# Experts' slabs of 1024 columns, down rows in pairs, and weight splits emitted ahead in a hybrid attention and mixture-of-experts kernel

## The chip, the cores and the metric

The kernel runs on one core of one Trainium2 chip. The metric is device time in microseconds (us), the median of three runs. All times below are us unless marked ns.

## The reference

Two layers over 256 tokens of width 1024, in float32. Layer 0 is an attention of two kinds of heads and a SwiGLU of width 2816. Layer 1 is a gated MLP and a mixture of 8 experts with 2 experts per token. Each half layer ends in a residual sum and a layer norm. The change is in the experts:

```python
D_MODEL = 1024; SEQ = 256; N_EXPERTS = 8; TOP_K = 2; D_FF_EXPERT = 3584
...
logits = (xf @ w_router).astype(jnp.float32)
top_val, top_idx = lax.top_k(logits, TOP_K)
gate = jax.nn.softmax(top_val, axis=-1)
...
def expert_block(args):
    xb, e = args
    return (jax.nn.silu(xb @ w_gate[e]) * (xb @ w_up[e])) @ w_down[e]
...
contrib = yb[dest] * g_sorted[:, None].astype(yb.dtype)
y = jnp.zeros((n_tok, dm), yb.dtype).at[tok_sorted].add(contrib)
```

`w_gate[e]` and `w_up[e]` have 1024 rows and 3584 columns, `w_down[e]` 3584 rows and 1024 columns: 336 MB (2^20 bytes each) of weights for the eight experts, all of which are read.

## The kernel before

Every weight is used as two float32r parts whose sum is the float32 value: `wh`, the rounded value, and `wl`, the rest. `weights` (L94) loads a tile of 128 partitions x 2048 floats (1 MB) into a raw buffer through SyncE's queue (L108), copies it to `wh` on the scalar engine, ACT (L123), and subtracts `wh` from it on the vector engine, DVE, or on GpSimd, POOL, to get `wl` (L127). `MOE_CUTS` (1, 1) does each in one instruction. Raw buffers form a ring: 4 in `stream`, 7 in `late`, 1 in `late2` and `W_BUFS_MOE` = 2 in the experts' pool, 14 in all; the first expert tiles also pass through the room of `xhl1` and `yacc` before these are needed. Split tiles form a ring of `WS_BUFS` = 3. An activation is split in the same way (`split_into`, L132: a copy on ACT, a subtraction on DVE), and each product becomes three on TensorE: high by high, high by low, low by high.

An expert has 128 slots for tokens. `gather` (L828) picks the tokens' rows with a 0/1 matrix (`take`) by products on TensorE, and splits them into `xh` and `xl`. The expert's 3584 hidden columns are worked in 7 slabs of 512. For each slab `expert_up` (L852) takes two tiles of gate weights and two of up weights (512 rows x 512 columns each) into one PSUM bank per matrix (`ps_a`, 4 banks), with tokens as the stationary operand; silu on ACT (L865) and a multiplication on DVE (L866) give `sg` [token, column]. `expert_turn` (L869) turns it with four transposes into a `ps_t` bank (2 banks) and splits it into `hh` and `hl` (`tag` with one buffer each). `expert_down` (L878) multiplies with two tiles of 256 rows of `w_down` into two banks that are kept for the whole expert; it runs one slab late, so that slab s + 1's gate and up products stand between the turn of slab s and its use.

After an expert's last slab `combine` (L895) splits the two banks into `y`, spreads them to the tokens' places with products L904 and L905 into `ps_t`, scales them on ACT into `part` (L910, one buffer of both token blocks) and adds them to `yacc` on POOL (L911). This stands in the middle of the next expert's first slab. The last expert adds on DVE instead and goes on into the last norm (`finish`).

Nothing sets an order by hand in this stage but the order of emission: each engine has one queue, a scheduler fills it at build time in order of emission as far as its own account of what is ready allows, and at run time each queue is worked strictly in its order. `run_experts` (L958) has the first two tiles split by POOL, and two more on DVE, while the router still works; `GATE_SLAB` = 3 and `GATHER_SLAB` = 5 say behind which slab the gate weights and the next expert's gather are emitted. A loop behind it (L999) treats experts with more tokens than slots; the trace shows no pass of it.

Of the kernel before, what the change touches and what calls it, by code (L numbers as in the profile page):

```python
# [17 lines left out]
P = 128  # L18
T = 256
# [15 lines left out]
W_BUFS, W_BUFS_LATE, W_BUFS_MOE, WS_BUFS = 4, 7, 2, 3  # L35
MOE_CUTS = (1, 1)
# the order of the attention's parts, and what takes the low parts of each part's weights: the vector engine or gpsimd
# [3 lines left out]
# how many of a group's four heads the scalar engine scales, for each block of queries  # L41
ASIDE = dict(a=(1, 1), w=(0, 1), s=(2, 1))
GATE_SLAB, GATHER_SLAB = 3, 5
# [7 lines left out]
def tile_hybrid_gmlp_moe(  # L51
# [23 lines left out]
    # weights: rings of 8 KB buffers (raw, and the two parts), spread over the pools that exist at the time  # L75
# [13 lines left out]
    def room(shape, dtype=F32):  # L89
        """a tile in the next buffer of the ring for raw weights"""  # L90
        pool, n = slot("w")
        return pool.tile(shape, dtype, name="w", tag="w", bufs=n)

    def weights(src, a, b, lo_engine=V, loads=1, cuts=(2, 4), behind=None):  # L94
        """src as two float32r parts whose sum is src; loaded and split in as many pieces as asked for, each equal
        share of the pieces queued behind what one entry of behind has for their engine."""
# [80 lines left out]
    def norm_rows(z, gb, state, to=None, done=None):  # L177
        """z [t, D], whose halves' statistics are in state -> its norm, in place or in to; done is called with each
        half after it."""
# [11 lines left out]
    def layer_norm(z, gb, accs=None, ready=None, done=None):  # L191
        """z [t, D] -> its norm, in place; with accs, z is first ALPHA * z plus the two halves in accs.
        ready is called with each half before the norm."""
# [9 lines left out]
    def mm_rows(accs, lhs_h, lhs_l, parts, first, last, done=None):  # L203
        """accs[b][half][t, 512] += x[:, k]^T w[k]; parts: (wh, wl, row chunks) of weight tiles, one block at a time."""
# [18 lines left out]
    def rows_2k(w, g, lo_engine=V):  # L223
        """rows g * 256 to g * 256 + 255 of a matrix of D columns"""
        return weights(w[g * 256:(g + 1) * 256, :].rearrange("(k p) c -> p k c", p=P), 2, D, lo_engine)
# [6 lines left out]
    def mm_cols(acc, lhs_h, lhs_l, w, js):  # L232
        """acc[col, t] = w[:, js]^T x, over the whole model dimension."""
# [13 lines left out]
    with ExitStack() as actx:  # L247
# [4 lines left out]
        # bias tables: -slope * distance, masked  # L252
# [7 lines left out]
        # compressed keys: token t against the last position of window c  # L260
# [14 lines left out]
        # sel[r, c] = 1 where r is c or c + 32: adds the two parts of a stacked product  # L275
# [41 lines left out]
        # softmax of one group of four heads over dense keys: probabilities times `scale4`, transposed  # L317
# [123 lines left out]
        # compression of k and v: two products around a gelu, for the 15 windows of each head  # L441
        def compress(lo_engines):
            for i, w1 in enumerate((cmp_wk1, cmp_wv1)):
# [16 lines left out]
                # gelu(z) = z / (1 + exp(-2 sqrt(2 / pi) (z + 0.044715 z^3)))  # L460
# [83 lines left out]
        # projections and attention, in the order that keeps the tensor engine fed  # L544
# [22 lines left out]
        # output projection, residual, norm  # L567
# [15 lines left out]
    with ExitStack() as fctx:  # L583
# [29 lines left out]
        def ffn_up_blocks(s):  # L613
            """the same, one block of tokens after the other"""
# [53 lines left out]
    with ExitStack() as gctx:  # L668
# [14 lines left out]
        # with the norm's gain and shift taken into the weights, it works from what the norm is taken of  # L683
# [42 lines left out]
        def route(b, zt, mv, rs):  # L726
            """zt: what the norm of this block is taken of, transposed"""
# [17 lines left out]
        def rank_tokens():  # L745
            """rank[t, b, e]: how many earlier tokens the expert has; -1 where the token isn't the expert's"""
# [69 lines left out]
    # the ring goes on in what was the last layer's; the room of the sums takes a weight tile first  # L816
# [11 lines left out]
    def gather(n, take):  # L828
        """the rows of x that the slots take, transposed and split; and the way back, [slot, t]"""
# [16 lines left out]
    n_slab = FE // 512  # L846

    def up_weights(w, s, kh, *how, **kw):
        src = w[kh * 512:(kh + 1) * 512, s * 512:(s + 1) * 512]
        return weights(src.rearrange("(k p) c -> p k c", p=P), 4, 512, *how, **kw)  # L850

    def expert_up(w_gate, w_up, s, xh, xl, ready):  # L852
        pss = []
        for w in (w_gate, w_up):
            acc = ps_a()
            for kh in range(2):
                wh, wl = ready.pop(0) if ready else up_weights(w, s, kh, cuts=MOE_CUTS)
                for i in range(4):
                    k = 4 * kh + i
                    PE.matmul(acc, xh[:, k, :], wh[:, i, :], start=k == 0, stop=False)  # L860
                    PE.matmul(acc, xh[:, k, :], wl[:, i, :], start=False, stop=False)  # L861
                    PE.matmul(acc, xl[:, k, :], wh[:, i, :], start=False, stop=k == KD - 1)  # L862
            pss.append(acc)
        sg = moe.tile([P, 512], F32, name="sg", tag="sg", bufs=1)
        S.activation(sg, pss[0], AF.Silu)  # L865
        V.tensor_tensor(sg, sg, pss[1], op=OP.mult)  # L866
        return sg
# [175 lines left out]
```

## Time and profile before

| | us |
|---|---|
| median of three runs (lowest, highest) | 1482.59 (1481.17, 1483.14) |
| the profiled execution: its span, from its first to its last instruction (the time known of it) | 1480.9 |
| TensorE products busy | 1426.8 (96%) |
| DVE busy | 1182.6 (80%) |
| ACT busy | 953.0 (64%) |
| POOL busy | 174.3 (12%) |

One execution was profiled. Its span is 1.7 us below the median. "Busy" of TensorE (PE) is the time in which at least one product is under way; products overlap, and their ends are modelled, so the pace must be read from starts. PEld is the load of the stationary operand, which runs beside the products. A queue row (SPq) is the issue of a DMA, not its transfer. The first expert's products start at 448 us, the last product of the kernel at 1464.8 us.

### The profile page before, as it was taken

How to read it: one execution, taken by the hardware profiler on the slowest of the kernel's cores; microseconds unless marked ns; L12 is line 12 of the kernel's file. 1: busy time of each engine (PE TensorE's matmuls, PEld its weight loads, DVE VectorE, ACT ScalarE, POOL GpSimd, SP SyncE). 2: the span in 40 equal slices, each digit the busy share in tenths (PEclk: the TensorE clock that was granted, in tenths of full speed). 3: DMA queues.
4: the chain of work that ended last, by engine and by line, in shares of the span. 5: the costliest groups of instructions: out<-in, count | busy, mean ns of one | idle time of the engine just before them, and what ended most of it. 6: DMA issues, size and time to landing. Idle time of an engine off the chain costs nothing. (4 is left out here: it accounts for less than half of the span.)

```text
span 1480.9 us, 18693 instructions
## 1 busy us (share of the span) xinstructions
PE 1426.8 (96%) x7207; PEld 1186.0 (80%) x7207; DVE 1182.6 (80%) x1265; ACT 953.0 (64%) x920; POOL 174.3 (12%) x139
## 2 busy tenths in 40 slices
PE   8899999999979999999999999999999999999995
PEld 7887899997768887888788788878878887887883
DVE  7888855558667988888888888888888878888886
ACT  5677544443436767776776777777677667767772
POOL 8521100002050101000200200020020002002000
PEclk9999999999989999999999999999999999999998
DMA  9523975556558898999999999999999999999940
GB/s 274 175 88 98 351 261 185 198 171 214 179 190 295 313 358 312 358 364 329 328 364 342 330 351 361 346 328 368 339 325 365 363 335 331 363 351 323 353 191 31
DMA packets 198847, 425.72 MB, mean 287 GB/s; under 512 B 8472, under 2 KB 44368, under 8 KB 198752
## 3 DMA queue, kind: packets, MB, share of 16 engines
q1 hardware_dynamic: 196448, 419.71, 80.2%
q0 software_dynamic: 1248, 4.24, 1.0%
q8 instruction: 58, 0.95, 0.3%
q10 hardware_dynamic: 1056, 0.53, 0.1%
q14 instruction: 37, 0.30, 0.1%
HBM read 423.40 MB, written 1.05 MB: 287 GB/s over the span
## 5 line engine op out<-in xcount | busy, mean ns | idle before, releaser
L127 DVE TENSOR_TENSOR wl<-w,wh 128x2048 fp32r<-128x2048 f32 (+1 forms) x544 | 907.4, 1696 | 189.3 <-ACT wh L123 185.8
L123 ACT CAST wh<-w 128x2048 fp32r<-128x2048 f32 (+1 forms) x462 | 766.5, 1668 | 255.9 <-PE ps_a L862 102.3
L860 PE MATMUL ps_a<-wh,xhl 128*128 128x512 f32 x896 | 356.4, 398 | 0.0
L862 PE MATMUL ps_a<-wh,xhl 128*128 128x512 f32 x896 | 354.4, 396 | 0.0
L861 PE MATMUL ps_a<-wl,xhl 128*128 128x512 f32 x896 | 354.2, 395 | 0.0
L862 PEld LDWEIGHTS ps_a<-wh,xhl 128*128 128x128 f32 x896 | 168.4, 188 | 39.5
L861 PEld LDWEIGHTS ps_a<-wl,xhl 128*128 128x128 f32 x896 | 168.5, 188 | 38.5
L860 PEld LDWEIGHTS ps_a<-wh,xhl 128*128 128x128 f32 x896 | 168.4, 188 | 38.6
L892 PE MATMUL ps_d<-wl,hh 128*128 128x512 f32 x448 | 178.8, 399 | 0.0
L893 PE MATMUL ps_d<-wh,hl 128*128 128x512 f32 x448 | 176.8, 395 | 0.0
L891 PE MATMUL ps_d<-wh,hh 128*128 128x512 f32 x448 | 167.7, 395 | 0.4 <-ACT hh L133 0.4
L911 POOL TENSOR_TENSOR yacc<-yacc,part 128x512 f32<-128x512 f32 x28 | 65.4, 2356 | 796.9 <-ACT part L910 796.9
L236 PE MATMUL ps_a<-xth,wh 128*128 128x256 f32 x448 | 128.6, 288 | 3.1 <-DVE hg L471 3.1
L238 PE MATMUL ps_a<-xth,wl 128*128 128x256 f32 x448 | 128.5, 287 | 0.8 <-DVE wl L127 0.8
L237 PE MATMUL ps_a<-xtl,wh 128*128 128x256 f32 x448 | 127.7, 285 | 0.0
L891 PEld LDWEIGHTS ps_d<-wh,hh 128*128 128x128 f32 x448 | 84.2, 188 | 20.9 <-ACT hh L133 0.9
L892 PEld LDWEIGHTS ps_d<-wl,hh 128*128 128x128 f32 x448 | 84.3, 188 | 20.1 <-DVE wl L127 1.4
L893 PEld LDWEIGHTS ps_d<-wh,hl 128*128 128x128 f32 x448 | 84.3, 188 | 18.5
L236 PEld LDWEIGHTS ps_a<-xth,wh 128*128 128x128 f32 x448 | 86.5, 193 | 4.9 <-issue 3.7
L238 PEld LDWEIGHTS ps_a<-xth,wl 128*128 128x128 f32 x448 | 86.5, 193 | 2.5 <-issue 1.2
L237 PEld LDWEIGHTS ps_a<-xtl,wh 128*128 128x128 f32 x448 | 86.5, 193 | 0.9 <-DVE xtl L134 0.2
L127 POOL TENSOR_TENSOR wl<-w,wh 128x512 fp32r<-128x512 f32 (+1 forms) x56 | 65.8, 1209 | 69.8 <-ACT wh L123 69.7
(304 smaller groups left out, 1377.9 us busy)
## 6 DMA issues: line engine op xcount, KB each, us to landing
w<-in_moe_w_gate_dram SPq DMA_DIRECT2D x112, 1024.0 KB, 6.3
w<-in_moe_w_up_dram SPq DMA_DIRECT2D x112, 1024.0 KB, 7.3
w<-in_moe_w_down_dram SPq DMA_DIRECT2D x112, 1024.0 KB, 6.8
w<-in_ffn_w_gate_dram SPq DMA_DIRECT2D x11, 1024.0 KB, 5.6
w<-in_ffn_w_up_dram SPq DMA_DIRECT2D x11, 1024.0 KB, 9.3
w<-in_ffn_w_down_dram SPq DMA_DIRECT2D x11, 1024.0 KB, 6.2
w<-in_gmlp_w_in_dram SPq DMA_DIRECT2D x8, 1024.0 KB, 5.1
w<-in_att_w_in_dram SPq DMA_DIRECT2D x7, 1024.0 KB, 6.0
```

The source lines that it names most:

```text
L123: S.copy(wh_f[:, sl], w_f[:, sl])
L127: ins = lo_engine.tensor_tensor(wl_f[:, sl], w_f[:, sl], wh_f[:, sl].bitcast(F32), op=OP.subtract)
L236: PE.matmul(acc, wh[:, k, js], lhs_h[:, k, :], start=k == 0, stop=False)
L237: PE.matmul(acc, wh[:, k, js], lhs_l[:, k, :], start=False, stop=False)
L238: PE.matmul(acc, wl[:, k, js], lhs_h[:, k, :], start=False, stop=k == KD - 1)
L860: PE.matmul(acc, xh[:, k, :], wh[:, i, :], start=k == 0, stop=False)
L861: PE.matmul(acc, xh[:, k, :], wl[:, i, :], start=False, stop=False)
L862: PE.matmul(acc, xl[:, k, :], wh[:, i, :], start=False, stop=k == KD - 1)
L891: PE.matmul(accs[half], hh[:, k, :], wh[:, i, hs], start=s == 0 and k == 0, stop=False)
L892: PE.matmul(accs[half], hh[:, k, :], wl[:, i, hs], start=False, stop=False)
L893: PE.matmul(accs[half], hl[:, k, :], wh[:, i, hs], start=False, stop=last and k == 3)
L911: G.tensor_tensor(yacc[:, b, hs], yacc[:, b, hs], part[:, b], op=OP.add)
```

## The change

The hidden columns of an expert are worked in slabs of 1024, 1024, 1024 and 512 columns. A gate or up tile of a wide slab holds 256 rows of 1024 columns, four tiles per matrix, and its products go to two PSUM banks, so that a wide slab uses all four `ps_a` banks. Silu, multiplication, transposes and splits of `hh` and `hl` are done once per 512 columns, as before, in tiles of twice the size. A down tile holds 256 rows of which partition p has rows 2p and 2p + 1, next to each other in memory, in place of p and 128 + p; the transposes therefore take every second column of `sg`. The three products of a row chunk come in the order high by high, low by high (both with `wh`), high by low. All tiles of all experts stand in one list (`order`), and `take_tile` emits loads and splits until three tiles are ready before it gives out the next, where before a tile's load and split were emitted just ahead of its own products. The raw ring has one buffer fewer; three tiles instead of four are split ahead of the first expert; only the very last tile is cut into pieces, instead of the last two; `GATE_SLAB` and `GATHER_SLAB` become 1 and 2, and `yacc` is set up together with the gate weights. Layer 0, the gated MLP, the router, `combine` and `finish` are unchanged but for comments.

```diff
-W_BUFS, W_BUFS_LATE, W_BUFS_MOE, WS_BUFS = 4, 7, 2, 3
+W_BUFS, W_BUFS_LATE, W_BUFS_MOE, WS_BUFS = 4, 7, 1, 3
-GATE_SLAB, GATHER_SLAB = 3, 5
+GATE_SLAB, GATHER_SLAB = 1, 2
...
-    n_slab = FE // 512
-
-    def up_weights(w, s, kh, *how, **kw):
-        src = w[kh * 512:(kh + 1) * 512, s * 512:(s + 1) * 512]
-        return weights(src.rearrange("(k p) c -> p k c", p=P), 4, 512, *how, **kw)
-
-    def expert_up(w_gate, w_up, s, xh, xl, ready):
-        pss = []
-        for w in (w_gate, w_up):
-            acc = ps_a()
-            for kh in range(2):
-                wh, wl = ready.pop(0) if ready else up_weights(w, s, kh, cuts=MOE_CUTS)
-                for i in range(4):
-                    k = 4 * kh + i
-                    PE.matmul(acc, xh[:, k, :], wh[:, i, :], start=k == 0, stop=False)
-                    PE.matmul(acc, xh[:, k, :], wl[:, i, :], start=False, stop=False)
-                    PE.matmul(acc, xl[:, k, :], wh[:, i, :], start=False, stop=k == KD - 1)
-            pss.append(acc)
-        sg = moe.tile([P, 512], F32, name="sg", tag="sg", bufs=1)
-        S.activation(sg, pss[0], AF.Silu)
-        V.tensor_tensor(sg, sg, pss[1], op=OP.mult)
+    slabs = [(c0, min(1024, FE - c0)) for c0 in range(0, FE, 1024)]
+    def up_src(w, s, i):
+        c0, wd = slabs[s]
+        a = 2048 // wd
+        return w[i * a * P:(i + 1) * a * P, c0:c0 + wd].rearrange("(k p) c -> p k c", p=P), a, wd
+    def down_src(w, s, i):
+        r0 = slabs[s][0] + i * 256
+        return w[r0:r0 + 256, :].rearrange("(p i) c -> p i c", i=2), 2, D
+    def expert_up(take_tile, s, xh, xl):
+        wd = slabs[s][1]
+        a, n_half = 2048 // wd, wd // 512
+        accs2 = []
+        for m in range(2):
+            accs = [ps_a() for _ in range(n_half)]
+            for i in range(KD // a):
+                wh, wl = take_tile()
+                for j in range(a):
+                    k = a * i + j
+                    for h, acc in enumerate(accs):
+                        hs = slice(h * 512, (h + 1) * 512)
+                        PE.matmul(acc, xh[:, k, :], wh[:, j, hs], start=k == 0, stop=False)
+                        PE.matmul(acc, xl[:, k, :], wh[:, j, hs], start=False, stop=False)
+                        PE.matmul(acc, xh[:, k, :], wl[:, j, hs], start=False, stop=k == KD - 1)
+            accs2.append(accs)
+            if m == 0:
+                sg = moe.tile([P, 1024], F32, name="sg", tag="sg", bufs=1)
+                for h, acc in enumerate(accs):
+                    S.activation(sg[:, h * 512:(h + 1) * 512], acc, AF.Silu)
+        for h, acc in enumerate(accs2[1]):
+            hs = slice(h * 512, (h + 1) * 512)
+            V.tensor_tensor(sg[:, hs], sg[:, hs], acc, op=OP.mult)
         return sg
 
-    def expert_turn(sg):
-        pt = ps_t()
-        for i in range(4):
-            PE.transpose(pt[:, i * P:(i + 1) * P], sg[:, i * P:(i + 1) * P], ident)
-        hh = moe.tile([P, 4, P], F32R, name="hh", tag="hh", bufs=1)
-        hl = moe.tile([P, 4, P], F32R, name="hl", tag="hl", bufs=1)
-        split_into(hh, hl, pt.rearrange("p (k t) -> p k t", t=P))
+    def expert_turn(sg, s):
+        hh = moe.tile([P, 8, P], F32R, name="hh", tag="hh", bufs=1)
+        hl = moe.tile([P, 8, P], F32R, name="hl", tag="hl", bufs=1)
+        for g in range(slabs[s][1] // 512):
+            pt = ps_t()
+            for c in range(4):
+                cols = sg[:, (2 * g + c // 2) * 256:(2 * g + c // 2 + 1) * 256].rearrange("p (t j) -> p j t", j=2)
+                PE.transpose(pt[:, c * P:(c + 1) * P], cols[:, c % 2, :], ident)
+            split_into(hh[:, 4 * g:4 * g + 4], hl[:, 4 * g:4 * g + 4], pt.rearrange("p (k t) -> p k t", t=P))
         return hh, hl
 
-    def expert_down(w_down, s, hh, hl, accs, closing):
-        last = s == n_slab - 1
-        parts = []
-        for kh in range(2):
-            r0 = s * 512 + kh * 256
-            parts.append((kh, *weights(w_down[r0:r0 + 256, :].rearrange("(k p) c -> p k c", p=P), 2, D,
-                                       cuts=(2, 4) if closing and last else MOE_CUTS)))
-        for grp, half in [(parts, 0), (parts, 1)] if last else [([p], h) for p in parts for h in range(2)]:
-            hs = slice(half * 512, (half + 1) * 512)
-            for kh, wh, wl in grp:
-                for i in range(2):
-                    k = 2 * kh + i
-                    PE.matmul(accs[half], hh[:, k, :], wh[:, i, hs], start=s == 0 and k == 0, stop=False)
-                    PE.matmul(accs[half], hh[:, k, :], wl[:, i, hs], start=False, stop=False)
-                    PE.matmul(accs[half], hl[:, k, :], wh[:, i, hs], start=False, stop=last and k == 3)
+    def expert_down(take_tile, s, hh, hl, accs):
+        last = s == len(slabs) - 1
+        n = slabs[s][1] // 256
+        got = [(i, *take_tile()) for i in range(n)] if last else [None] * n
+        for grp, hf in [(got, 0), (got, 1)] if last else [([i], h) for i in range(n) for h in range(2)]:
+            hs = slice(hf * 512, (hf + 1) * 512)
+            if not last:
+                if hf == 0:
+                    cur = (grp[0], *take_tile())
+                grp = [cur]
+            for i, wh, wl in grp:
+                for j in range(2):
+                    k = 2 * i + j
+                    PE.matmul(accs[hf], hh[:, k, :], wh[:, j, hs], start=s == 0 and k == 0, stop=False)
+                    PE.matmul(accs[hf], hl[:, k, :], wh[:, j, hs], start=False, stop=False)
+                    PE.matmul(accs[hf], hh[:, k, :], wl[:, j, hs], start=False, stop=last and k == 2 * n - 1)
 
...
     def run_experts(todo, start_acc):
-        ready = [up_weights(todo[0][0], 0, kh, G, cuts=(2, 8), behind=[after[kh]]) for kh in range(2)] if start_acc else []
+        order = []
+        behind = None
+        for n, (w_gate, w_up, w_down, _, _) in enumerate(todo):
+            for s in range(len(slabs)):
+                order += [up_src(w, s, i) for w in (w_gate, w_up) for i in range(slabs[s][1] // 256)]
+                if behind:
+                    order += behind
+                behind = [down_src(w_down, s, i) for i in range(slabs[s][1] // 256)]
+        order += behind
+        ready = []
+        at = [0]
+        def fetch(*how, **kw):
+            if at[0] < len(order):
+                src, a, b = order[at[0]]
+                at[0] += 1
+                if at[0] == len(order):
+                    kw["cuts"] = (2, 4)
+                ready.append(weights(src, a, b, *how, **{"cuts": MOE_CUTS, **kw}))
+        def take_tile():
+            while len(ready) < WS_BUFS and at[0] < len(order):
+                fetch()
+            return ready.pop(0)
+        if start_acc:
+            for i in range(2):
+                fetch(G, cuts=(2, 8), behind=[after[i]])
         take = take_of(todo[0][3])
-        ready += [up_weights(todo[0][1], 0, kh, cuts=MOE_CUTS, behind=[marks]) for kh in range(2)] if start_acc else []
+        if start_acc:
+            fetch(behind=[marks])
         gathered = [gather(0, take)]
         late_down = None
         for n, (w_gate, w_up, w_down, rank_of, gate_of) in enumerate(todo):
             closing = n == len(todo) - 1
             xh, xl, back = gathered[n]
-            for s in range(n_slab):
-                sg = expert_up(w_gate, w_up, s, xh, xl, ready)
+            for s in range(len(slabs)):
+                sg = expert_up(take_tile, s, xh, xl)
                 if late_down:
                     late_down()
                 if s == 0:
                     accs = [ps_d(), ps_d()]
-                hh, hl = expert_turn(sg)
+                hh, hl = expert_turn(sg, s)
                 if s == GATE_SLAB and n == 0 and start_acc:
                     gate_weights()
-                if s == 4 and n == 0 and start_acc:
                     yacc = held["yacc"] = moe.tile([P, NB, D], F32, name="yacc", tag="yacc", bufs=1)
                     for b in range(NB):
                         with tc.issue_after(marks[G].ins):
...
                 if s == GATHER_SLAB and not closing:
                     gathered.append(gather(n + 1, take_of(todo[n + 1][3])))
 
-                def late_down(n=n, w=w_down, s=s, hh=hh, hl=hl, accs=accs, back=back, gate_of=gate_of, closing=closing):
-                    expert_down(w, s, hh, hl, accs, closing)
-                    if s == n_slab - 1:
+                def late_down(n=n, s=s, hh=hh, hl=hl, accs=accs, back=back, gate_of=gate_of, closing=closing):
+                    expert_down(take_tile, s, hh, hl, accs)
+                    if s == len(slabs) - 1:
                         combine(n, accs, back, gate_of, finish() if closing else None)
         late_down()
```

## Rows read from the trace of the kernel before

**Rows 1.** Busy time by stretch: engine busy (instructions), granted clock, DMA share, GB/s.

```profile
448.00:1465.00 1017.00, 1008.67 (x4562) 816.07 (x4560) 859.66 (x504) 726.62 (x515) 71.24 (x30) 1.00 0.92 329
500.00:520.00 20.00, 20.00 (x91) 16.20 (x90) 17.29 (x13) 14.72 (x11) 0.00 (x0) 1.00 1.03 373
```

**Rows 2.** Groups of instructions in 448 to 1465 us, shapes apart: busy us, mean ns.

```profile
L127 DVE TENSOR_TENSOR wl<-w,wh 128x2048 fp32r<-128x2048 f32 x331 | 764.9, 2325 | 125.7 <-ACT wh L123 125.0
L123 ACT CAST wh<-w 128x2048 fp32r<-128x2048 f32 x331 | 632.4, 1911 | 160.8 <-PE ps_a L862 101.5 <-PE ps_d L893 56.7 <-issue 2.2
L860 PE MATMUL ps_a<-wh,xhl 128*128 128x512 f32 x896 | 356.4, 398 | 0.0
...
L892 PE MATMUL ps_d<-wl,hh 128*128 128x512 f32 x448 | 178.8, 399 | 0.0
...
L911 POOL TENSOR_TENSOR yacc<-yacc,part 128x512 f32<-128x512 f32 x28 | 65.4, 2356 | 796.9 <-ACT part L910 796.9
L866 DVE TENSOR_TENSOR sg<-sg,ps_a 128x512 f32<-128x512 f32 x56 | 38.3, 685 | 23.4 <-PE ps_a L862 23.3
L134 DVE TENSOR_TENSOR hl<-ps_t,hh 128x512 fp32r<-128x512 f32 x56 | 38.2, 682 | 0.5 <-ACT hh L133 0.5
...
L865 ACT ACTIVATE sg<-ps_a 128x512 f32<-128x512 f32 x56 | 33.7, 601 | 49.5 <-PE ps_a L862 49.5
...
L835 PE MATMUL ps_t<-take,x_nat 128*128 128x128 f32 x224 | 27.5, 276 | 0.0
L872 PEld LDWEIGHTS ps_t<-ident,sg 128*128 128x128 f32 x224 | 27.4, 140 | 16.7 <-ACT part L910 9.6 <-DVE sg L866 0.3
...
L910 ACT ACTIVATE part<-ps_t,gate 128x512 f32<-128x512 f32 x28 | 17.8, 688 | 8.9 <-POOL yacc L911 8.9
L904 PE MATMUL ps_t<-y,back 128*128 128x512 f32 x32 | 12.2, 407 | 1.3 <-DVE yacc L907 1.3
```

**Rows 3.** Timeline, TensorE, 725 to 745 us: start, duration, instruction.

```profile
725.97 0.40 PE L891 MATMUL ps_d<-wh,hh 128*128 128x512 f32 x1
...
731.55 0.60 PE L872 MATMUL ps_t<-ident,sg 128*128 128x128 f32 x4
731.90 0.48 PE L860 MATMUL ps_a<-wh,xhl 128*128 128x512 f32 x1
```

**Rows 4.** Timeline, TensorE, end of a down product of layer 0.

```profile
183.86 0.39 PE L645 MATMUL ps_d<-wh,hh 128*128 128x512 f32 x1
...
186.66 0.28 PE L236 MATMUL ps_a<-xth,wh 128*128 128x256 f32 x1
```

**Rows 5.** Waits of weight loads, 448 to 1465 us: total, times, longest.

```profile
PEld ps_t L872 <- ACT part L910: 9.6, 7, 1.4
PEld ps_d L892 <- DVE wl L127: 1.4, 9, 0.2
...
PEld ps_t L835 <- DVE hl L134: 0.7, 2, 0.3
```

**Rows 6.** Waits of SyncE, which issues the loads, 448 to 1465 us.

```profile
SPq L108 <- DVE wl L127: 829.4, 316, 11.1
```

**Rows 7.** DMA issues: count, KB each, median us from issue to landing.

```profile
w<-in_moe_w_up_dram SPq DMA_DIRECT2D x112, 1024.0 KB, 7.3
```

**Rows 8.** Timeline, all engines, after the `combine` of the second expert.

```profile
716.31 0.40 PE L861 MATMUL ps_a<-wl,xhl 128*128 128x512 f32 x1
716.83 1.27 ACT L910 ACTIVATE part<-ps_t,gate 128x512 f32<-128x512 f32 x2 [1.32 <-POOL yacc L911]
...
717.57 0.66 PE L872 MATMUL ps_t<-ident,sg 128*128 128x128 f32 x4 [0.86 <-ACT part L910]
```

**Rows 9.** Timeline, all engines, a steady slab: the tightest tile.

```profile
738.25 1.90 ACT L123 CAST wh<-w 128x2048 fp32r<-128x2048 f32 x1
...
740.18 4.60 DVE L127 TENSOR_TENSOR wl<-w,wh 128x2048 fp32r<-128x2048 f32 x2 [0.99 <-ACT wh L123]
...
743.37 0.40 PE L892 MATMUL ps_d<-wl,hh 128*128 128x512 f32 x1
```

## Prediction

> **What bounds the kernel now.** I read the 40 slices and the stretch of the experts first. The experts take 448 to 1465 us, two thirds of the span, so everything that this change touches lies there. [...] The DMA engines are shown busy 92 to 103%, which looks like a second bound. It isn't: the view of SyncE's waits [rows 6] says that 316 of the 336 weight loads were issued only when the vector engine had freed a raw buffer. The 14 buffers are always full and the loads queue for room, not the arithmetic for loads.
>
> A busy TensorE is not a TensorE at its peak, so I worked out its pace from starts. Twenty-four down products with nothing between them start from 725.97 to 731.55 us [rows 3]: 5.58 / 24 = 0.2325 us each. The experts issue 3 x 896 + 3 x 448 = 4032 such products (L860 to L862, L891 to L893; [rows 2] shows one line of each kind): 4032 x 0.2325 = 937.4 us. To this come the gather's 27.5 us of busy time and 64 products of `combine` (L904 and L905, 32 each, [rows 2]), 64 x 0.2325 = 14.9. The 224 transposes L872 come in 56 groups of four, and a group holds TensorE for 731.90 - 731.55 = 0.35 us [rows 3]: 56 x 0.35 = 19.6. Sum 999 of 1017 us. Everything that a better order could still win is 18 us, 1.2% of the kernel. The view of the waits of weight loads [rows 5] names most of it: 9.6 us in 7 places, where the first transposes after a `combine` wait for a `ps_t` buffer that `part` (L910) must empty first. Waiting for a split weight comes to 1.4 us in 9 places, waiting before the gather to 0.7 us in two.
>
> **The change part by part.**
>
> *Products.* A wide slab has 2 x 8 x 2 x 3 = 96 gate and up products and 4 x 2 x 2 x 3 = 48 down products; three wide slabs and one narrow (48 + 24) make 3 x 144 + 72 = 504 per expert and 4032 in all, as before, of the same shape. Their order changes: both products that need only `wh` come first. Layer 0's down products have that order already, with other DMA traffic about, and 12 of them take 186.66 - 183.86 = 2.80 us [rows 4], 0.2333 each against 0.2325. Cost: 0.
>
> *Splits, silu, product, turn.* 336 tiles of 2048 columns are still split by one copy (1.91 us) and one subtraction (2.33 us); silu, multiplication, `hh` and `hl` stay at 56 pieces of 512 columns each [rows 2]. Nothing is saved on either engine, and neither bounds: 0. The one tile at the end that is no longer cut in pieces delays nothing but itself. In the tail `hl` is wanted one product earlier than before; its subtraction takes 0.68 us [rows 2], so 0 to 0.7 us; I take 0.5.
>
> *Splits emitted ahead.* Up to three split tiles exist before and after (`WS_BUFS` is 3), so a split can't begin before TensorE has let go of the tile three back. Emission ahead moves the splits in the queues of ACT and DVE, not in time. What it can change is the cover: how long a low part lies ready before its first use. In a steady slab before, the tightest tile is the one behind silu: its copy starts at 738.25, the subtraction at 740.18 runs 2.29 us to 742.47, and the first product that reads it starts at 743.37 [rows 9]: 0.90 us of cover. After the change two silus stand in front of such a copy (another 0.60 us, [rows 2]) and the low part is wanted one product later (0.23 us): 0.90 - 0.60 + 0.23 = 0.53 us left. Behind the two multiplications and the two `hl` (0.68 us more on DVE each) tiles with 1.4 us of cover or more follow, which keep 0.9. So no stall: 0. If two such pairs hit one tile the cover is gone; this is priced below.
>
> *Down rows in pairs.* Partition p holds rows 2p and 2p + 1, so the hidden columns must be turned with a step of two floats. The 224 transposes remain; their stationary operand `sg` is read at every second float. No row of before reads a stationary operand at such a step. Bounds: 0 below, since nothing less is loaded; above, a group twice as long, 56 x 0.35 = 19.6 us more [rows 3]. I take 0, by the nearest row, the load of the same 128 columns of four bytes at step one, 140 ns [rows 2]. [...]
>
> *Loads.* Rows get longer (2 KB to 4 KB for gate and up, and 8 KB in one piece for down). Loads wait for buffers, so faster ones land earlier and lie longer. The ring of raw tiles drops from 14 to 13 (`W_BUFS_MOE`). TensorE takes a tile every 12 x 0.2325 = 2.8 us, so 13 tiles are 36 us ahead, and a load needs 7.3 us to land [rows 7]. Cost: 0, with some 29 us of cover. SyncE's queue issues the same 336 loads in the order in which they are used.
>
> *Start and gather.* Three tiles are split before the first expert instead of four; but the fourth had to wait for the first one's buffer anyway. `gate_weights` and `yacc` keep their place after as many products (two wide slabs against four narrow). 0.
>
> *`combine`.* Its chain is unchanged: `part` of the second half waits for POOL's two additions (2.36 us each, [rows 2]), which free the one `part` buffer; then `part` frees `ps_t`, then the transposes may go. In the trace [rows 8] the last product before them starts at 716.31 and they start at 717.57: 717.57 - 716.31 - 0.23 = 1.03 us idle, and `part` starts at 716.83 after waiting for POOL. Behind the transposes in TensorE's order stand the next slab's products, which could have run. The splits now come ahead of `combine` in the emission, but the two that do are of tiles whose buffers come free at the same moments as before, so I expect the same queue on ACT. New: a wide turn needs both `ps_t` buffers, the second freed by one more `part`, 0.69 us later [rows 2]. Between 0 and 7 x 0.69 = 4.8 us more; I take 0, since products can stand between the groups, and 7 x 1.03 = 7.2 us is what could go.
>
> Sum: 1480.9 + 0.5 = 1481.4 us for the profiled execution; the median of the runs shown is 1482.6, 1.7 above that span, so 1483.1, and I say 1483.
>
> **The rivals.** *A, faster: the stall after `combine` goes.* Splits emitted ahead could let the order put more products of the next slab before the transposes. It is worth 7 x 1.03 = 7.2 us: 1483 - 7 = 1476 us; the whole wait of [rows 5], 9.6 us, gives 1473. For it speaks that the products are there to be run; against it that `part`, POOL and the `ps_t` ring are the same.
>
> *B, slower: the second group waits.* A wide turn takes both `ps_t` buffers. After each `combine` that is up to 4.8 us in all; and the gather, which now follows a wide turn, needs the same buffers, each freed by an `hl` of 0.68 us, 7 x 0.68 = 4.8 us. Together 1483 + 9.6 = 1493 us. It decides from the point where the transposes or the gather stand in TensorE's order before the buffers are free. Against it: before the gather only 0.7 us in two places are waited for now [rows 5].
>
> *C, slower: the cover of the splits is used up.* If the second silu and the second multiplication fall on one tile, 0.60 + 0.69 - 0.23 = 1.06 us stand against 0.90 of cover: 0.16 us late, in two places of each of 24 wide slabs: 8 us, 1491. It decides from 0.9 us of extra delay.
>
> *D, slower: the turned columns are read at half pace.* 19.6 us more on the engine that sets the end: 1503. For it speaks that no row reads a stationary operand at a step; against it that 128 columns of four bytes remain what is loaded.
>
> *E: longer DMA rows make it faster.* This would be so if loads were waited for; [rows 6] says the reverse. It gives no change, 1483.
>
> **How the numbers follow.** A measurement of this kernel can tell about 0.2%, 3 us, from no change. No change, E with it: 0.45 (own range 1480 to 1486). A, in part or whole, more than 3 us: 0.25. B and C: 0.20. D: 0.06. The rest, 0.04, is divided between the two sides. So faster 0.27, same 0.45, slower 0.28. The range from 1474 to 1495 us takes in A nearly whole, B and C, and leaves out D and the rest, about 0.1, and the extremes of A and C.
>
> **What would show each step.** In the profile after: 4032 products at 0.2325 us; LDWEIGHTS of the turned `sg` near the 140 ns of before (D: near 280); SyncE's loads still waiting for DVE; weight loads waiting for `part` 7 times, with 1 us each (A: none; B: 14 times, or a new row before the gather); waits of products for `wl` at a few us in all (C: 8 us or more). I would be wrong if the order of TensorE's queue after `combine` comes out differently, since it sets the only idle time that is worth having, or if packing `hh` in one tile of twice the size holds up something that I took for free.

## The result: 24 us slower

The changed kernel takes 1506.9 us (median of 4 runs, 1505.9 to 1507.8), the kernel before 1482.9 beside it: a ratio of 1.0164 (95%: 1.0149 to 1.0178). The prediction was 1483, with a range to 1495: wrong. The profiled execution has a span of 1505.7 us against 1480.9, at the same granted clock of 0.986.

First the parts that came as predicted. The stretch of the experts in the changed kernel, busy time by engine (columns as in [rows 1]):

```profile
448.00:1490.00 1042.00, 1017.16 (x4566) 820.11 (x4565) 854.35 (x505) 724.35 (x514) 70.03 (x30) 1.00 0.88 322
```

Its groups by line in that stretch (as in [rows 2]):

```profile
L127 DVE TENSOR_TENSOR wl<-w,wh 128x2048 fp32r<-128x2048 f32 x332 | 759.8, 2311 | 144.4 <-ACT wh L123 144.3
L123 ACT CAST wh<-w 128x2048 fp32r<-128x2048 f32 x332 | 632.0, 1912 | 182.9 <-PE ps_a L872 111.2 <-PE ps_d L911 68.7 <-issue 2.1
L871 PE MATMUL ps_a<-wh,xhl 128*128 128x512 f32 x896 | 354.9, 396 | 0.0
...
L912 PE MATMUL ps_d<-wl,hh 128*128 128x512 f32 x448 | 170.5, 398 | 0.0
...
L892 PEld LDWEIGHTS ps_t<-ident,sg 128*128 128x128 f32 x224 | 32.7, 206 | 10.2 <-ACT part L929 7.6
```

And the landing of its loads (as in [rows 7]):

```profile
w<-in_moe_w_up_dram SPq DMA_DIRECT2D x112, 1024.0 KB, 5.5
```

The counts are the same, and so are the durations of products and splits. Loads land sooner (5.5 us instead of 7.3) and nobody needs it. Only the load of the turned `sg` at step two is longer: 206 ns instead of 140.

What was lost stands in the waits. First TensorE's in the changed kernel, 448 to 1495 us (the total in us, how often, the longest):

```profile
PE ps_a L873 <- DVE wl L127: 16.7, 15, 1.5
PE ps_t L892 <- ACT part L929: 4.5, 7, 0.9
PE ps_t L835 <- DVE hl L134: 1.6, 8, 0.2
PE ps_t L923 <- DVE yacc L926: 1.3, 2, 0.8
PE ps_d L910 <- ACT hh L133: 0.7, 1, 0.7
```

Then ACT's waits there from the fourth expert on, 880 to 1495 us:

```profile
ACT hh L133 <- PE ps_d L912: 44.1, 11, 4.0
...
ACT sg L878 <- PE ps_a L873: 31.5, 14, 3.2
```

The first line of TensorE's waits has no counterpart in the kernel before: there weight loads waited for `wl`, 1.4 us in 9 places [rows 5], but no product did. Its largest line was (448 to 1465 us):

```profile
PE ps_t L872 <- ACT part L910: 6.5, 7, 1.0
```

None of the 15 waits for `wl` in the changed kernel lies before 880 us. By the timeline, from the last product ahead of the first transposes after one `combine` to that of the next are 127.5 us at first (600.14 to 727.67) and 132.3 us later (988.87 to 1121.14). So the first three experts run about as fast as before, and each later one loses 4.8 us. In two lines of ACT's waits the single wait has grown. `hh` used to wait for the down products 21 times, 1.1 us each on average, and silu for the gate products 50 times, 1.0 us each, as these lines of the kernel before show (448 to 1465 us):

```profile
ACT hh L133 <- PE ps_d L892: 23.8, 21, 2.0
ACT sg L865 <- PE ps_a L862: 49.5, 50, 2.1
```

Now `hh` waits 11 times, 4.0 us each, and silu up to 3.2 us. In the kernel before these waits, 73.3 us in the two lines, held up no product for `wl`. What one of them can do is seen in the timeline of the changed kernel, in a slab of the fourth expert (start, duration, instruction):

```profile
882.99 1.91 ACT L123 CAST wh<-w 128x2048 fp32r<-128x2048 f32 x1 [1.72 <-PE ps_d L911]
...
888.72 0.40 PE L871 MATMUL ps_a<-wh,xhl 128*128 128x512 f32 x1
888.91 0.59 ACT L133 CAST hh<-ps_t 128x512 fp32r<-128x512 f32 x1 [4.01 <-PE ps_d L912]
889.40 1.91 ACT L123 CAST wh<-w 128x2048 fp32r<-128x2048 f32 x1
...
891.34 2.29 DVE L127 TENSOR_TENSOR wl<-w,wh 128x2048 fp32r<-128x2048 f32 x1 [1.11 <-ACT wh L123]
892.22 0.40 PE L872 MATMUL ps_a<-wh,xhl 128*128 128x512 f32 x1
893.69 0.72 PE L873 MATMUL ps_a<-wl,xhl 128*128 128x512 f32 x2 [1.08 <-DVE wl L127]
```

`hh` has one buffer, which the last down product of the slab before (it starts at 888.49) still reads. So ACT stands idle for 4.01 us in front of `hh`. The split behind it starts at 889.40, its subtraction ends at 891.34 + 2.29 = 893.63, and TensorE, whose next product was due at 892.22 + 0.23 = 892.45, starts it at 893.69: 1.24 us late. Twelve us later the same happens behind silu, which waits 3.22 us for the last gate product. Worked out from the starts of successive products (their distance less the pace of 0.23 us), there are 14 such stalls of 1.24 us, one of 1.71 in the last expert, and 0.73 us (in two parts) beside each of four gathers: 17.4 + 1.7 + 2.9 = 22 us.

### The profile page after: what moved, and what is told of

It reads as the page before. It is cut to its first block, busy times and chain, and to the rows that moved or that the text cites. A ratio compares the mean times of both kernels' runs of the same rounds, so it can differ in the third digit from the quotient of the medians.

```text
span 1505.7 us, 18670 instructions
## 1 busy us (share of the span) xinstructions
PE 1434.2 (95%) x7207; PEld 1189.1 (79%) x7207; DVE 1179.2 (78%) x1262; ACT 950.5 (63%) x919; POOL 173.5 (12%) x139
## 5 line engine op out<-in xcount | busy, mean ns | idle before, releaser
L873 PE MATMUL ps_a<-wl,xhl 128*128 128x512 f32 x896 | 344.0, 398 | 16.7 <-DVE wl L127 16.7
L910 PE MATMUL ps_d<-wh,hh 128*128 128x512 f32 x448 | 176.8, 395 | 0.7 <-ACT hh L133 0.7
L912 PE MATMUL ps_d<-wl,hh 128*128 128x512 f32 x448 | 170.5, 398 | 0.0
```

The costliest lines, as they stand in the source:

```text
L873: PE.matmul(acc, xh[:, k, :], wl[:, j, hs], start=False, stop=k == KD - 1)
L910: PE.matmul(accs[hf], hh[:, k, :], wh[:, j, hs], start=s == 0 and k == 0, stop=False)
L912: PE.matmul(accs[hf], hh[:, k, :], wl[:, j, hs], start=False, stop=last and k == 2 * n - 1)
```

## Experiments

Theory 1, formed on this timeline: an instruction of ACT that must wait for TensorE stands in ACT's queue in front of splits that could already run; it is this place that costs. Theory 2: the turned columns at step two cost (rival D). Theory 3: the emission ahead, or the wide slab with its two silus, makes splits late by itself.

**The place in ACT's queue.** The changed kernel, with silu and the split of `hh` queued behind the latest split copy:

```diff
-                S.copy(wh_f[:, sl], w_f[:, sl])
+                marks["wh"] = S.copy(wh_f[:, sl], w_f[:, sl])
...
-                    S.activation(sg[:, h * 512:(h + 1) * 512], acc, AF.Silu)
+                    with tc.issue_after(marks["wh"].ins):
+                        S.activation(sg[:, h * 512:(h + 1) * 512], acc, AF.Silu)
...
+            with tc.issue_after(marks["wh"].ins):
+                split_into(hh[...], hl[...], ...)
```

> The changed kernel, with silu and the hh copies tied in ACT's queue behind the last weight split that is emitted before them; nothing else differs. Theory 1 (from the fourth expert on the queue has hh and silu in front of splits that could already run; each waits 3 to 4 us for TensorE at the end of a 48-product stretch, the low part comes 1.24 us late, some 15 times, and the gather waits a little): the waits for wl fall from 17 us to under 3, time about 1487 us. Theory 2 (turning columns at a step of two floats costs the time): no change, 1507. Theory 3 (two silus and two hh per wide slab are simply too long for the cover, in whatever order): the waits stay, 1503 to 1507.

Measured: 1483.7 us, ratio 1.0005 (0.9996 to 1.0015). Here and below the ratio is to the kernel before, measured beside each version, and its 95% interval follows. The whole loss is gone, within that interval. The same slab in its timeline:

```profile
885.96 1.91 ACT L123 CAST wh<-w 128x2048 fp32r<-128x2048 f32 x1 [0.99 <-PE ps_d L913]
...
887.90 2.29 DVE L127 TENSOR_TENSOR wl<-w,wh 128x2048 fp32r<-128x2048 f32 x1 [0.60 <-ACT wh L123]
888.99 1.08 ACT L133 CAST hh<-ps_t 128x512 fp32r<-128x512 f32 x2 [1.12 <-PE ps_d L914]
```

The split that stood behind `hh` now starts at 885.96 instead of 889.40, 3.44 us earlier, and `hh` itself loses nothing: 888.99 against 888.91. Its buffer comes free when it does. That the split was released by TensorE at 885.96 shows that it was ready while ACT stood idle in the changed kernel. DVE's order changed with ACT's (both `hl` now stand behind this subtraction), but in the changed kernel DVE stood idle for ACT's copy, 1.11 us just before the late subtraction, so `hl` was not what held it.

**The step of two.** The changed kernel with rows and columns at step one, and the kernel before with rows in pairs and columns at step two:

```diff
-        return w[r0:r0 + 256, :].rearrange("(p i) c -> p i c", i=2), 2, D
+        return w[r0:r0 + 256, :].rearrange("(k p) c -> p k c", p=P), 2, D
...
-                PE.transpose(pt[:, c * P:(c + 1) * P], cols[:, c % 2, :], ident)
+                PE.transpose(pt[:, c * P:(c + 1) * P], sg[:, (4 * g + c) * P:(4 * g + c + 1) * P], ident)
```

> The changed kernel with down tiles of rows p and 128 + p again and transposes of columns next to each other. Theory 1: the queues keep their order and the waits for wl stay; only the transposes get shorter, 224 by some 18 ns: 4 us, time about 1503. Theory 2: the whole loss goes, 1483 to 1487. Theory 3: as theory 1, 1503.

> The kernel before with only the down rows in pairs, and so with transposes at a step of two floats. Theory 1: 4 us for 224 transposes, and less where they stand beside waits: about 1487. Theory 2: most of the loss is here, 1500 to 1507. Theory 3: 1487.

Measured: 1504.9 us (1.0155, 1.0138 to 1.0172), with 16.7 us of waits for `wl` as in the changed kernel; and 1483.6 us (1.0008, 0.9999 to 1.0018). Theory 2 falls as the cause: by these two runs the step is worth 2.0 and 0.7 us of the 24, and neither difference is clear of its interval.

**Emission ahead and the rest, in narrow slabs.**

```diff
-    slabs = [(c0, min(1024, FE - c0)) for c0 in range(0, FE, 1024)]
+    slabs = [(c0, min(512, FE - c0)) for c0 in range(0, FE, 512)]
...
-GATE_SLAB, GATHER_SLAB = 1, 2
+GATE_SLAB, GATHER_SLAB = 3, 5
```

> The changed kernel with slabs of 512 columns, all else kept: emission ahead, row pairs, order of products, 13 raw buffers, gate weights and gather behind the fourth and sixth slab as before. Theory 1: hh and silu may still stand before splits, but the stretch that they wait for is half as long, so a wait of 1 to 2 us fits the cover: waits for wl under 3 us, time about 1487, the 4 us over the kernel before being the transposes. Theory 2: no change, 1507. Theory 3: single silus and hh fit the cover, 1487; so this one tells theory 2 apart, not 3.

Measured: 1539.1 us (1.0387, 1.0370 to 1.0405), a miss of all three theories: slower still, so the loss doesn't need the wide slabs. TensorE's waits in it, 448 to 1530 us:

```profile
PE ps_a L873 <- DVE wl L127: 24.7, 16, 1.6
PE ps_t L892 <- ACT part L929: 19.8, 7, 3.6
```

And ACT's:

```profile
ACT hh L133 <- PE ps_d L912: 91.9, 21, 4.4
...
ACT part L929 <- POOL yacc L930: 21.7, 7, 3.8
```

`hh` stands early here in every slab from the fourth expert on. After `combine`, TensorE's first transposes wait for the second pair of `part`, and this for POOL's two additions to `yacc`, which take 6.08 us where they take 3.58 in the narrow version of the next experiment (start, duration; first here, then there):

```profile
842.81 6.08 POOL L930 TENSOR_TENSOR yacc<-yacc,part 128x512 f32<-128x512 f32 x2 [118.92 <-ACT part L929]
841.85 3.58 POOL L930 TENSOR_TENSOR yacc<-yacc,part 128x512 f32<-128x512 f32 x2 [117.83 <-ACT part L929]
```

Why the additions take longer was not tested. By the starts, the 55 us over that version are mostly 16 stalls of 1.7 us, five of 3.76 us in place of 1.1, and a fall of the clock, shown at three of these five (last section). Three things were left that could set these places: the order of the products, the emission ahead, the width. The next three runs take them one by one.

**The old order of the products**, in wide and in narrow slabs (the down products likewise):

```diff
-                        PE.matmul(acc, xl[:, k, :], wh[:, j, hs], start=False, stop=False)
-                        PE.matmul(acc, xh[:, k, :], wl[:, j, hs], start=False, stop=k == KD - 1)
+                        PE.matmul(acc, xh[:, k, :], wl[:, j, hs], start=False, stop=False)
+                        PE.matmul(acc, xl[:, k, :], wh[:, j, hs], start=False, stop=k == KD - 1)
```

> The changed kernel with one thing undone: within a row chunk the products run hh x wh, hh x wl, hl x wh again, as before (for gate and up the same with xh and xl). Wide slabs, rows in pairs and splits emitted ahead all stay. Theory 1 (an instruction of ACT that waits for TensorE stands in its queue ahead of splits whose buffers are free; it is the position that costs): the written order of ACT's queue comes out with both hh copies behind all of the down stretch's splits, so hh should wait about 1 us instead of 4 us, the waits of products for wl should fall from 16.7 us to a few, and the time should be 1483 to 1487 us. Rival: the emission ahead or the wide slabs themselves make the splits late, whatever the product order: 1505 to 1508 us, with the waits for wl as in the changed kernel.

> The narrow form of the changed kernel (slabs of 512 columns, which took 1539 us), with the product order of before as the only further difference. The written order of ACT's queue is then that of the kernel before in the steady slabs. Theory 1: the 21 waits of hh for the down products (4.4 us each in the narrow form) fall to about 1 us, the waits for wl and for part go back to what before showed, and the time is 1483 to 1488 us. Rival (emission ahead is what costs, and more so in narrow slabs): it stays above 1510 us.

Measured: wide 1495.0 us (1.0084, 1.0068 to 1.0099), narrow 1484.0 us (1.0013, 1.0003 to 1.0022). In narrow slabs the product order accounts for all of the 55 us; the emission ahead, which that version keeps, costs next to nothing there. In wide slabs it accounts for 12 of the 24 us, so the expectation of 1483 to 1487 missed. ACT's view tells why: `hh` has no long wait left, but silu has:

```profile
ACT sg L878 <- PE ps_a L873: 38.6, 31, 3.0
```

and TensorE has 9 stalls of 1.0 us, two for each expert from the fourth on and one for the last. Ahead of the fourth expert the first silu of eleven slabs stands one split copy earlier than in the first experiment, too, and no stall follows. The waits are short there (448 to 880 us):

```profile
ACT sg L878 <- PE ps_a L873: 5.0, 13, 1.7
```

So it is the long wait at the early place that costs, not the place by itself.

**One kind of instruction held at a time.** The order of ACT's instructions can be counted. Against the first experiment, which has no such stall, each expert of the changed kernel from the fourth on has the silus of two wide slabs (in the last expert: of one) one split copy earlier, and the first `hh` of two wide slabs one earlier; all else has its place (but for the last expert's final `hh`, which is two earlier). If one place costs one stall, holding either kind must give back its own share. The edits are those of the first experiment, for `hh` alone and for silu alone.

> The changed kernel with only the hh and hl splits held behind the latest split in ACT's queue; silu stays where the changed kernel had it. Counting split copies in the written queue against the first experiment (no stalls), every hh is then in the same place, while from the fourth expert on both silus of two of the three wide slabs stand one split earlier. Theory (one place too early costs one stall of 1.24 us on TensorE): the 10 stalls behind silu stay, the 5 behind hh, the shorter ones around the gather and the 1.7 us in the last expert go: 1483.7 + 10 x 1.24 = 1496 us, waits for wl from 16.7 to about 11 us. Rival (one wait makes the next, so that holding either kind is enough): 1484 to 1487 us. Rival (holding hh alone does nothing, since the silu wait would come instead): 1505 to 1507 us.

> The counterpart: only silu is held behind the latest split, hh and hl stay where the changed kernel had them (from the fourth expert on the first hh of two wide slabs of each expert stands one split earlier than in the first experiment). Theory: the 10 stalls behind silu go; 5 of 1.24 us and one of 1.7 us behind hh stay, and 5 x 0.73 us around the gather: 1483.7 + 6.2 + 1.7 + 3.7 = 1495 us. The two gains together then make up the whole loss. Rivals as for the run before: 1484 to 1487 us, or 1505 to 1507 us.

Measured: 1495.1 us (1.0087, 1.0070 to 1.0104) and 1495.6 us (1.0082, 1.0065 to 1.0099), where 1496 and 1495 were expected (with 10 stalls behind silu; the last expert has one such slab, so there are 9). TensorE's first line of waits with `hh` held:

```profile
PE ps_a L873 <- DVE wl L127: 9.9, 9, 1.1
```

And with silu held:

```profile
PE ps_a L873 <- DVE wl L127: 6.9, 6, 1.5
```

9.9 + 6.9 = 16.8 us, the 16.7 of the changed kernel; by the starts, 9 stalls of 1.25 us are left in the one, 5 of 1.24, the one of 1.71 and those of the gathers in the other. The two gains, about 11.5 us each, make up the loss.

**Emission on demand.**

```diff
-            while len(ready) < WS_BUFS and at[0] < len(order):
+            while len(ready) < 1 and at[0] < len(order):
```

> The changed kernel with the splits emitted on demand again (one tile ahead instead of three); the wide slabs, the rows in pairs and the new product order stay. In the written queue of ACT the same silus as in the changed kernel stand one split early from the fourth expert on, and both halves of the same hh splits instead of the first alone. Theory (place in the queue): no gain, 1503 to 1509 us. Rival (emission ahead is what makes splits late, as the change's third part): 1483 to 1488 us.

Measured: 1511.9 us (1.0194, 1.0177 to 1.0211). The rival (1483 to 1488) is out: without emission ahead the splits are late all the same, and with it, in the first experiment, they are not. So theory 3 falls. The time lies 3 us above what I gave and 5 us above the changed kernel; 17.0 us of waits for `wl` are there as expected. Of the 5 us, six places where a product starts 0.33 us late for `wh` make 2.0, and a fall of the clock in the last expert, shown in the last section, some 1.4; the rest stays open.

**A version that beats both.** With the queue mended, what is left in the experts is the wait after `combine`. The turn of an expert's first slab is moved behind the second gate tile of the next slab:

```diff
-    def expert_up(take_tile, s, xh, xl):
+    def expert_up(take_tile, s, xh, xl, mid=None):
...
-                        PE.matmul(acc, xh[:, k, :], wl[:, j, hs], start=False, stop=k == KD - 1)
+                        mm = PE.matmul(acc, xh[:, k, :], wl[:, j, hs], start=False, stop=k == KD - 1)
+                if mid and m == 0 and i == 1:
+                    with tc.issue_after(mm.ins):
+                        mid()
...
-                hh, hl = expert_turn(sg, s)
+                turned = []
+                if s == 0 and n > 0:
+                    mid = lambda sg=sg, s=s, to=turned: to.extend(expert_turn(sg, s))
+                else:
+                    turned.extend(expert_turn(sg, s))
```

> A version meant to beat both kernels: the changed kernel with silu and hh held behind the latest split in ACT's queue (as in the first experiment), the down rows and the turned columns as before the change (step one), and the turn of an expert's first slab moved, on TensorE, behind the second tile of the next slab's gate products, so that it no longer stands in front of products that could run while part and the additions of the combine step go on. Theory (rival A of the prediction, now made on purpose): the seven waits of the first transposes for part, 7.5 us in all, go, and the step of two costs 1 to 2 us: 1483.7 - 7.5 - 1.5 = 1475 us, range 1473 to 1478. Rival (the wait is only moved: to the later turn, to the hidden parts that come later, or to the splits behind them): 1480 to 1484 us.

> The kernel before with that last move alone: the turn of an expert's first slab (n > 0) behind the next slab's gate products on TensorE. Theory: the 9.6 us of weight loads that wait for part shrink to under 2 us and the time falls from 1482.9 to 1475 to 1477 us. Rival: the wait is only moved: 1481 to 1484 us.

> The first experiment (silu and hh held behind the latest split) with the down rows and the turned columns at step one again; it is the version of the seventh experiment without the moved turn, and splits that one's gain in two. Expected by the 4.1 us that the trace of the changed kernel shows for 224 transposes at step two, and the 2 us that the time of the second experiment gained: 1483.7 - 2 to 4 = 1480 to 1482 us; the moved turn is then worth 1.5 to 3.5 us and not 7. Rival: the step costs nothing in the time (1483.5), and the turn was worth 5.

Measured: 1478.4 us (0.9971, 0.9959 to 0.9983) for the changed kernel with silu and `hh` held, step one and the moved turn, just above the range given; 1482.0 us (0.9995, 0.9986 to 1.0005) for the same without the moved turn; 1481.8 us (0.9997, 0.9988 to 1.0006) for the kernel before with the move alone. So the step of two is worth 1483.7 - 1482.0 = 1.7 us (the two intervals overlap; with the 2.0 and 0.7 above, all three differences point the same way) and the moved turn 1482.0 - 1478.4 = 3.6. I had expected 7.5 for the turn, from the waits of weight loads; the products' own waits for `part` without the move are 4.6 us, which is nearer to what came (448 to 1495 us):

```profile
PE ps_t L892 <- ACT part L930: 4.6, 7, 0.9
```

In the kernel before, the same move gains nothing that the interval can tell. Its waits of weight loads with the move (448 to 1495 us):

```profile
PEld ps_a L861 <- DVE wl L127: 5.6, 11, 0.7
PEld ps_d L895 <- DVE wl L127: 4.6, 12, 0.7
```

Those of the fast version:

```profile
PEld ps_a L873 <- DVE wl L127: 5.8, 12, 0.5
```

The wait for `part` is gone in both and waits for `wl` come instead. By the starts of products, the fast version has 12 gaps of 0.15 to 0.27 us, 2.5 in all, in place of seven of 0.7 to 1.0, 5.7 in all; in the kernel before more comes through to the products: 14 gaps of about 0.4 us and four of 0.2, 6.2 in all, in place of seven of 1.0 to 1.2, 7.7 in all.

## Why the prediction was wrong

*The step that failed* is this one, of the splits emitted ahead: "Emission ahead moves the splits in the queues of ACT and DVE, not in time ... So no stall: 0." I asked when a split's buffers come free, and took each silu and `hh` for a delay of its own length, 0.60 us. I never asked how long it may wait while a ready split stands behind it, and took it that each instruction keeps its place in ACT's queue. The runs put 3.2 to 4.0 us of waiting there, and 23 us in the time: what the first experiment gave back. At the place of the timeline above the split came 3.44 us later, of which 2.2 us were cover and 1.24 reached TensorE. The row to read was in the profile: ACT's waits of `hh` and silu for TensorE. One place earlier made them three to four times the 1.0 and 1.1 us that they were on average. ACT did not pass over the waiting instruction: in the timeline above it stood idle for 4.01 us with a ready split behind.

The cover was also read at the wrong place. The slab of [rows 9], 0.90 us at 738 us, is one of the third expert, and not the tightest: in the nine places of [rows 5] a weight load already waited for `wl`. In the kernel before, too, `hh` waits for the down products almost only from the fourth expert on, 20 times of the 21 (880 to 1465 us):

```profile
ACT hh L133 <- PE ps_d L892: 22.7, 20, 2.0
```

The term of the *products*, "Cost: 0", failed by the same road. They keep their pace (eleven in a row from 899.63 to 902.19 us in the changed kernel, 0.233 us each), but their new order was worth 12 of the 24 us in wide slabs and all of the 55 in narrow ones, through the places in ACT's queue.

*Rival C* named the right place, the split behind silu, and its own point of decision, 0.9 us of extra delay; 3.44 us came. Its mechanism, two instructions by their lengths, gave 0.16 us in 48 places; it was 1.24 us in 14, 1.71 in one and 0.73 beside four gathers, behind silu and behind `hh` alike. *The range* ended at 1495, below the result: a queue order that I could not see was priced as if it stayed.

*Step of two:* I took 0 and had bounds of 0 and 19.6; it is 0.7 to 2 us. *`combine`:* TensorE's waits for `part` fell from 6.5 to 4.5 us, so 2 us of rival A came by themselves; a second group of transposes waits for nothing, so this half of rival B is out. Its other half came in part: the gather waited for `hl`, 1.6 us in 8 places by the line above and 2.9 us by the starts, and with `hh` held that line is gone, so it came from the same places in the queue. *The tail* lost some tenths, as allowed for. *Loads* (rival E) were right: SyncE's queue still waits for room, 317 times for DVE, as its line of the waits of the changed kernel shows (448 to 1490 us, beside [rows 6]):

```profile
SPq L108 <- DVE wl L127: 853.9, 317, 9.8
```

What stays open is why the queue is written otherwise. With the old products narrow slabs come out well and wide ones do not; with the new ones neither does, and in wide slabs emission on demand doesn't change that. The kernel before with the new order of products alone, or with wide slabs alone, was not run, so whether one of the two is enough is not shown. The place is chosen when the program's instruction streams are made, and no run here shows by what.

## What to carry to other kernels

Before an edit of order is costed at nothing, look in the waits of each engine for instructions that wait for the bounding engine, and ask what becomes of the ready work behind them if one of them stands one place earlier. Where such a place matters, fix it by an explicit edge in the code; here three lines were worth 23 us. Read cover in every stretch of the kernel and not in one early slab: here the waits differed from the fourth expert on. And price a stall of TensorE from its products' own row of waits, not from its weight loads', as an upper bound: here the weight loads' row gave 7.5 us, the products' 4.6, and the moved turn gained 3.6, with waits for `wl` in place of those for `part`.

## What was not expected of the hardware

The load of the turned `sg`, read at every second float, took 206 ns instead of 140 ([rows 2] and the group above); with step one again, in the second experiment, it took 140. The busy time of the 224 loads rose from 27.4 to 32.7 us, and the time of the kernel by 0.7 to 2 us. The prediction took the 140 ns of step one for it, and so 0; the row of the changed kernel says that the step is not free.

The narrow version showed a slower pace behind long stalls. After the first of the five stalls of 3.76 us in which TensorE waited for `part` (from 845.67 to 849.66 us, less the pace), its products are 0.43 us apart up to 852.72 us and then 0.23 again. The stretches before, at and after it (columns as in [rows 1]; the last three are granted clock, DMA share and GB/s):

```profile
838.00:845.00 7.00, 6.74 (x30) 5.06 (x29) 4.94 (x4) 5.84 (x6) 2.19 (x1) 1.00 0.85 300
850.40:852.70 2.30, 2.30 (x7) 1.83 (x6) 0.69 (x1) 2.06 (x2) 1.81 (x2) 0.50 0.82 319
853.00:860.00 7.00, 7.00 (x32) 5.63 (x31) 5.24 (x5) 5.54 (x4) 0.00 (x0) 1.00 0.50 169
```

The granted clock is 0.50 in the second. Around two more of the five it is 0.83 on average (980 to 1000 and 1120 to 1130 us). The stalls of 1.24 us in the changed kernel leave it at 1.00, as the stretch around one of them shows, first below. The length of a stall does not settle it: in the version with emission on demand two stalls of 0.33 and 1.76 us in the last expert, 0.9 us apart, are followed by 0.50, as the second line shows, while the single stall of 1.71 us in the changed kernel, at 1458 us, is not (granted clock 1.00 from 1455 to 1462 us).

```profile
890.00:896.00 6.00, 4.92 (x22) 3.65 (x21) 4.89 (x4) 5.78 (x5) 0.00 (x0) 1.00 0.70 229
1463.90:1466.30 2.40, 2.40 (x7) 1.90 (x6) 2.40 (x2) 0.00 (x0) 0.00 (x0) 0.50 0.03 7
```
